# Attention slots of two units: score products on 64-row halves of the array, transposes head by head between filler

## The chip, the cores and the metric

The kernel runs on one core of a Trainium2 chip. The metric is the device time of one execution in microseconds. TensorE (PE) multiplies, with weight loads as instructions of their own (PEld); VectorE (DVE), ScalarE (ACT) and GpSimd (POOL) are the other engines with work; SP, ACT and POOL issue the DMAs. Each engine works through its instructions in their written order and waits on semaphores for the others.

## The reference

One layer on 2048 tokens (a grid of 32 rows by 64 columns) of width 1024: RMSNorm with adaptive shift and scale, one input projection, then two branches whose outputs are joined, projected, gated, added to the input and normalised again. The change is in the neighbourhood attention: 8 heads of 64, and for every token a window of 8 rows by 16 columns of keys.

```
s = jnp.einsum('bhrcd,bhrjkd->bhrcjk', qg, kg) + bias     # scores and relative position bias
s = jnp.where(col_mask[:, None, :], s, -jnp.inf)
p = jax.nn.softmax(s over all keys of the window)
o = jnp.einsum('bhrcjk,bhrjkd->bhrcd', p, vg)
na_out = o * jax.nn.silu(na_z)                             # the gate
out = concatenate([na_out, ml_out]) @ w_out
```

## The kernel before

The program has three stages: the input projections of values and gates with the tables of biases; the mLSTM passes, with the remaining projections (`nq_gen`: z, keys, queries) as filler between their steps; and `phase2`, the attention with the output projection as filler. The fp32 products are made from a high and a low part of each operand: high x high, high x low and low x high.

In `phase2` the tokens are cut into 16 patches of 128 queries (8 rows by 16 columns). A unit is a patch and two heads (`ct`), so there are 64 units, four to a patch; its keys are 264 to 480. The order is written out by hand: `slot(n)` for n = 0 to 65 emits, one after the other, the scores of unit n (`stage_s`), the value products of unit n-2 (`stage_o`), the transposes of unit n-1 (`stage_t`), the loads, the scaling of unit n (`stage_n`) and then `pump(12)`: twelve steps of filler, first the last projections (`pq`), then the output projection of finished patches (`outproj`, tile `y`, 48 matmuls of 512 columns for each patch in two PSUM banks).

- Scores: for each of the two heads, two matmuls over 128 rows into one bank. `kk[ct]` holds, for head j, the high keys on its own 64 rows and the low keys on the other 64; `qhigh` holds the high queries on both halves (a second copy made by DMA, later by `double_q` on DVE), `qlow` the low ones on one half and zeros on the other.
- Softmax: DVE adds the bias table and takes the minimum (line 1346; tables hold the negative), ACT makes the exp with its sum (1347), DVE the reciprocal and the scaling (1356, 1358).
- Transposes: each head's chunks of keys are turned by TensorE into a bank of `pT` (1368; two banks), and ACT copies the bank to SBUF as `pt` (1370).
- Values: `pO` (1383), per chunk two matmuls with 64 columns of the array each, the two heads on the two halves of the output partitions; DVE gates the result into `zs` (1385).
- Output projection: `mix_high` on ACT (1393) and `mix_low` on DVE (1398) split the branch outputs; `y` (1420); DVE adds the residual (1425), ACT squares with a sum into the bank of y (1426), `scale` makes 1/rms with a dozen small DVE operations, `store` scales and writes out. The weights are loaded by `load_w` and split by `split_w` (1321 on ACT, 1322 on DVE) in the first slots (`first`).

PSUM's eight banks: 2 for the fillers (`pp`), 3 `pS`, 2 `pT`, 1 `pO`. The key projections for the lower half of the grid go straight into `kk` in `nq_gen` (885, 886: two ACT and two DVE operations each, on 64 rows), the others by way of DRAM (`kk_jobs`).

Of the kernel before, what the change touches and what calls it, by code (L numbers as in the profile page):

```python
# [62 lines left out]
class Kernel:  # L63
# [780 lines left out]
    def nq_gen(self):  # L844
# [10 lines left out]
        for i, s, g in order:  # L855
# [23 lines left out]
            if kind == "k" and g in lower:  # L879

                for j in range(2):
                    rows, other = slice(j * HD, (j + 1) * HD), slice((1 - j) * HD, (2 - j) * HD)
                    cols = slice(j * T + g * GT, j * T + (g + 1) * GT)
                    hv = self.kk[ct][rows, cols]
# [91 lines left out]
    def kk_jobs(self):  # L976

        flat = lambda t: t.rearrange("p a b -> p (a b)")
        self.kk = [flat(t) for g in (3, 2) for t in (self.hhi[g], self.hlo[g])]

        def load(ct, j, hl):
            src = self.d_kna[hl, ct * P + j * HD : ct * P + (j + 1) * HD, T // 2 :]
            row = j * HD if hl == 0 else (1 - j) * HD
            self.nc.sync.dma_start(self.kk[ct][row : row + HD, j * T + T // 2 : (j + 1) * T].bitcast(F32), src)

        return [[((3, 2)[ct // 2], lambda a=(ct, j, hl): load(*a)) for j in range(2) for hl in range(2)] for ct in range(4)]
# [67 lines left out]
    def ml_pass2(self, ml, h):  # L1054
# [11 lines left out]
        def load_z(gi):  # L1066
            while ("mz", h, gi) not in self.zdone:
                self.pump(1)
            if h == MH - 1 and gi == NG - 1:
                t = self.p2.tile([P, 4, P], F32, tag="pt", bufs=2, name="zt_last")  # L1070
            else:
                t = self.mle.tile([P, 4, CH], F32, tag="zt", bufs=1, name=f"zt_{h}_{gi}")
# [130 lines left out]
    def phase2(self):  # L1203
# [29 lines left out]
        qhigh = [p.tile([P, 2, 2, P], F32R, name=f"qhigh{i}") for i in range(3)]  # L1233
        qlow = [p.tile([P, 2, 2, P], F32R, name=f"qlow{i}") for i in range(3)]
# [14 lines left out]
        def load_q(i):  # L1249
# [3 lines left out]
            hi, lo = qhigh[i % 3], qlow[i % 3]  # L1253
            src = self.d_qna[0, c0 // 2, b].rearrange("(j p) c q -> p j c q", j=2)
            for rows in (slice(0, HD), slice(HD, P))[: 2 if i < 3 else 1]:
                (nc.gpsimd if i < 3 else nc.sync).dma_start(hi[rows].bitcast(F32), src)
            for j in range(2):
                js = slice(j * HD, (j + 1) * HD)
                (nc.gpsimd if i < 3 else nc.sync).dma_start(lo[js, j].bitcast(F32), self.d_qna[1, c0 // 2, b, js])

        def double_q(i):
            hi = qhigh[i % 3]
            nc.vector.tensor_copy(hi[HD:], hi[:HD].bitcast(F32))
# [63 lines left out]
        def stage_s(u):  # L1327
            b, ct = units[u]
            pr, pc, nr, nkc, nk, rpc, nch = geo[b]
            at, c = (u // 2) % 3, ct % 2  # L1330
            pts = []
            sums = few.tile([P, 2], F32, tag="sums", bufs=3, name=f"sums_{u}")
            scores = []
            rs = slice(PR_R0[pr], PR_R0[pr] + nr)
            cs = slice(PC_C0[pc], PC_C0[pc] + nkc)
            for j in range(2):
                ps = pS.tile([P, 512], F32, tag="pS", name=f"pS_{u}_{j}")[:, :nk]
                kv = kk[ct][:, j * T : (j + 1) * T].rearrange("p (r c) -> p r c", c=GRID_W)[:, rs, cs]
                o = ps.rearrange("p (r c) -> p r c", c=nkc)
                nc.tensor.matmul(o, qhigh[at][:, j, c, :], kv, start=True, stop=False)  # L1340
                nc.tensor.matmul(o, qlow[at][:, j, c, :], kv, start=False, stop=True)  # L1341
                scores.append(ps)
            for j, ps in enumerate(scores):
                pt = pbuf[(2 * u + j) % 4]
                mn = few.tile([P, 1], F32, tag="mn", bufs=4, name=f"mn_{u}_{j}")
                nc.vector.tensor_tensor_reduce(pt[:, :nk], ps, tabs[place[u]][j][:, :nk], 1.0, 3e38, ALU.add, ALU.min, mn)  # L1346
                nc.scalar.activation(pt[:, :nk], pt[:, :nk], AF.Exp, bias=mn, scale=-1.0, accum_out=sums[:, j : j + 1])  # L1347
                pts.append(pt)
                if u in follows:
                    load_tab(follows[u], j)  # L1350
            U[u] = (pts, sums)

        def stage_n(u):
# [3 lines left out]
            for j in range(2):  # L1357
                nc.vector.tensor_scalar(pts[j][:, :nk], pts[j][:, :nk], sums[:, j : j + 1], None, ALU.mult)

        def stage_t(u):  # L1360
            pr, pc, nr, nkc, nk, rpc, nch = geo[units[u][0]]
            cs = rpc * nkc
            pts, sums = U.pop(u)
            pT_sb = []
            for j in range(2):
                ps = pT.tile([P, 4, P], F32, tag="pT", name=f"pT_{u}_{j}")
                for i in range(nch):
                    nc.tensor.transpose(ps[:cs, i, :], pts[j][:, i * cs : (i + 1) * cs], self.ident)  # L1368
# [261 lines left out]
```

## Time and profile before

| | |
|---|---|
| median of 3 runs | 1390.58 us (1390.57 to 1395.54) |
| the profiled execution | 1391.12 us, span 1388.9 us |
| mean granted TensorE clock | 0.983 |
| busy: PE, PEld, DVE, ACT, POOL | 1309.5, 1126.1, 830.7, 528.2, 292.6 us |
| first scores | 1011.0 us |
| start of the last value products | 1358.4 us |

Times inside the profile are microseconds from the start of the span; the mean length of one instruction in a group is in ns. Matmul records are pipelined: their lengths overlap, so the distance of their starts is what one costs. A filler's group name (`y`, `pq`) is the tile that it writes.

### The profile page before, as it was taken

What the parts mean: (1) busy time and instruction counts of PE and PEld (TensorE: products, weight loads), DVE (VectorE), ACT (ScalarE), POOL (GpSimd) and SP (SyncE); (2) the same over time, 40 slices, a digit from 0 to 9 for tenths busy, and PEclk for the clock granted to TensorE, in tenths of its full rate; (3) what the DMA queues carried; (4) which work ended last, traced back from release to release, by engine and by line L of the source; (5) the groups of instructions that cost most, each with busy time, mean ns of one, the idle gap of its engine ahead of it and who ended that gap; (6) DMA issues with size and microseconds to landing.
All of it is one profiled execution on the core that took longest, in us unless ns stands there. A gap on an engine that the chain in (4) does not pass through costs nothing.

```text
span 1388.9 us, 23365 instructions
## 1 busy us (share of the span) xinstructions
PE 1309.5 (94%) x8052; PEld 1126.1 (81%) x8052; DVE 830.7 (60%) x2563; ACT 528.2 (38%) x1129; POOL 292.6 (21%) x321
## 2 busy tenths in 40 slices
PE   2989998998999999999999998999998999999996
PEld 2989998898887777888878887788876888888885
DVE  6683323111355569156867877877736777777674
ACT  4642334523222323213323313333345555555551
POOL 4453212424101010001212002212402111112111
PEclk9999999999999999999999999999999999999998
DMA  9798449788457675554776878846697897876862
GB/s 319 227 299 212 122 99 237 186 201 203 120 112 205 149 194 159 170 161 141 194 209 205 246 224 228 231 134 182 181 260 221 187 220 168 204 182 171 193 160 74
DMA packets 269707, 263.67 MB, mean 190 GB/s; under 512 B 33466, under 2 KB 230074, under 8 KB 269590
## 3 DMA queue, kind: packets, MB, share of 16 engines
q1 hardware_dynamic: 178062, 186.45, 50.5%
q0 software_dynamic: 21504, 37.73, 11.0%
q10 hardware_dynamic: 70024, 38.02, 9.7%
q8 instruction: 64, 1.05, 0.3%
q14 instruction: 53, 0.43, 0.1%
HBM read 177.57 MB, written 92.72 MB: 195 GB/s over the span
## 4 chain that ended last, share of the span: by engine, by line
PE 49%; DMA 8%; DVE 4%; issue 3%; ACT 1%; POOL 1%; POOLq 0%; ACTq 0%; SPq 0%; DVEq 0%
PE pq L865 19%; PE y L1420 10%; PE pO L1383 4%; PE pT L1368 3%; DMA tab<-d_t 2%; DMA kv<-d_ck 2%; PE pi L1093 2%; PE pc L429 2%; PE px L1091 2%; PE pc L430 2%; PE pc L431 2%; PE dc L1039 1%; PE pS L1341 1%; PE pS L1340 1%; DMA d_qna<-qst 1%
## 5 line engine op out<-in xcount | busy, mean ns | idle before, releaser
L865 PE MATMUL pq<-hhi,whi_a 128*128 128x512 f32 x512 | 208.7, 408 | 1.3 <-ACT u L773 0.8
L865 PE MATMUL pq<-hlo,whi_a 128*128 128x512 f32 x512 | 209.1, 408 | 0.0
L865 PE MATMUL pq<-hhi,wlo_a 128*128 128x512 f32 x512 | 208.4, 407 | 0.5 <-DVE wlo_a L842 0.5
L1347 ACT ACTIVATE pbuf<-pbuf,mn 128x480 f32<-128x480 f32 (+5 forms) x128 | 76.4, 598 | 105.5 <-DVE mn L1346 105.3
L865 PEld LDWEIGHTS pq<-hhi,whi_a 128*128 128x128 f32 x512 | 97.5, 190 | 19.2 <-ACT u L773 1.2
L865 PEld LDWEIGHTS pq<-hhi,wlo_a 128*128 128x128 f32 x512 | 97.5, 191 | 17.7 <-DVE wlo_a L842 1.0
L865 PEld LDWEIGHTS pq<-hlo,whi_a 128*128 128x128 f32 x512 | 97.5, 190 | 16.4
L1420 PE MATMUL y<-hhi,whi_a 128*128 128x512 f32 x256 | 85.8, 404 | 3.1 <-ACT hhi L1321 2.8
L1420 PE MATMUL y<-hhi,wlo_a 128*128 128x512 f32 x256 | 84.3, 399 | 0.0
L1346 DVE CUSTOM_DVE_ANT_0 pbuf<-pS,tab 128x480 f32<-128x480 f32 (+5 forms) x128 | 65.1, 541 | 29.3 <-PE pS L1341 19.4
L839 POOL TENSOR_TENSOR wlo_a<-rawq,whi_a 128x1024 fp32r<-128x1024 f32 x20 | 48.1, 2407 | 162.9 <-ACT whi_a L838 123.2
L1115 POOL TENSOR_TENSOR hm<-hm,ck 128x128 f32<-128x128 f32 x64 | 26.4, 412 | 263.3 <-DVE hm L1114 178.5
L429 PE MATMUL pvo<-whi_b,hhi 128*128 128x256 f32 x256 | 74.7, 292 | 7.2 <-DVE stvo L499 7.2
L1023 DVE TENSOR_SCALAR wv<-kv,gtile 128x129 f32<-128x129 f32 x120 | 37.9, 323 | 63.0 <-PE dc L1039 33.3
L1096 ACT ACTIVATE num<-px,gtile 128x129 f32<-128x129 f32 x120 | 38.3, 365 | 95.1 <-PE px L1091 75.3
L431 PE MATMUL pvo<-whi_b,hlo 128*128 128x256 f32 x256 | 73.6, 288 | 0.0
L430 PE MATMUL pvo<-wlo_b,hhi 128*128 128x256 f32 x256 | 73.6, 287 | 0.0
L499 DVE TENSOR_TENSOR stvo<-pvo,brow 128x256 f32<-128x256 f32 x64 | 26.5, 420 | 73.6 <-PE pvo L431 59.8
L714 ACT ACTIVATE dec<-dec,gtile 128x128 f32<-128x128 f32 x128 | 42.0, 392 | 69.7 <-POOL dec L710 52.2
L464 DVE TENSOR_TENSOR stv<-pv,brow 128x256 f32<-128x256 f32 x32 | 12.8, 423 | 85.4 <-DMA d_vna<-stv 38.8
L1383 PE MATMUL pO<-pt,v 128*64 128x128 f32 (+3 forms) x832 | 61.3, 283 | 0.5 <-ACT pt L1370 0.5
L1368 PE MATMUL pT<-ident,pbuf 128*128 128x128 f32 (+2 forms) x416 | 59.6, 282 | 0.0
(298 smaller groups left out, 3580.2 us busy)
## 6 DMA issues: line engine op xcount, KB each, us to landing
ck<-d_ck SPq DMA_DIRECT2D x64, 384.5 KB
kv<-d_ck SPq DMA_DIRECT2D x120, 128.5 KB
rawq<-in_w_main_dram SPq DMA_DIRECT2D x28, 512.0 KB
raw<-in_w_main_dram SPq DMA_DIRECT2D x20, 512.0 KB
d_ck<-stvo SPq DMA_DIRECT2D x16, 514.0 KB
x<-in_x_dram SPq DMA_DIRECT2D x16, 512.0 KB
wada<-in_w_ada_dram SPq DMA_DIRECT2D x32, 256.0 KB
dec<-d_mneg SPq DMA_DIRECT2D x32, 256.0 KB
```

What stands on the lines that cost most here:

```text
L429: nc.tensor.matmul(ps, lhi(k), rhi(k), start=(k == 0), stop=False)
L430: nc.tensor.matmul(ps, lhi(k), rlo(k), start=False, stop=False)
L431: nc.tensor.matmul(ps, llo(k), rhi(k), start=False, stop=(k == KT - 1))
L714: nc.scalar.activation(t[:, d, o, :], t[:, d, o, :], AF.Exp, bias=self.cols["g"][:, d, h, c : c + 1])
L839: nc.gpsimd.tensor_tensor(lo[:, :, cs], raw, hi[:, :, cs].bitcast(F32), ALU.subtract)
L865: nc.tensor.matmul(patch_ps(ps) if patch else ps, w, self.htok(h, g, k, patch), start=(k == 0 and n == 0), stop=(k == KT - 1 and n == 2))
L1096: nc.scalar.activation(num[:, d, :], px[:, d, :], AF.Copy, scale=self.cols["inter"][:, d, h, c : c + 1])
L1346: nc.vector.tensor_tensor_reduce(pt[:, :nk], ps, tabs[place[u]][j][:, :nk], 1.0, 3e38, ALU.add, ALU.min, mn)
L1347: nc.scalar.activation(pt[:, :nk], pt[:, :nk], AF.Exp, bias=mn, scale=-1.0, accum_out=sums[:, j : j + 1])
L1368: nc.tensor.transpose(ps[:cs, i, :], pts[j][:, i * cs : (i + 1) * cs], self.ident)
L1383: nc.tensor.matmul(po[j * HD : (j + 1) * HD, :], v[:n, h * HD : (h + 1) * HD], pt[j][:n, i, :], start=(i == 0), stop=(i == nch - 1))
L1420: nc.tensor.matmul(y, m[:, k, :], w[k][:, cs], start=(k == 4 and n == 0), stop=(k == 3 and n == 2))
```

## The change

Slots are of two units, `slot(m)` for m = 0 to 32. It emits the scores of units 2m and 2m+1, the value products of the two units before, both units' softmax, the loads, and then filler and the transposes of one head in turn: 6 filler steps, head, 5, head, 5, head, 4, head, 4 (10, 9, 9, 8, 8 in the first two). The scores are three products over 64 rows for each head, the two heads in turn on rows 0 to 63 and 64 to 127; `kk` and `qs` now hold the parts in plain order, high beside low on the free axis. The queries come by one DMA for each two units, without a second copy (`double_q` and the zeroed `qlow` go). Value products of both units write one bank and are gated by one operation. PSUM: 2 filler, 4 `pS`, 1 `pT`, 1 `pO`. The weight splits of the output projection move from slots 4 to 7 of one unit to slots 2 and 3 of two, four at a time, and the mixes are split where the second head of a pair slot has been turned. The lower keys are written by one ACT and one DVE operation on 128 rows.

```diff
@@ nq_gen
-                for j in range(2):
-                    rows, other = ...
-                    nc.scalar.activation(hv, ps[rows], AF.Identity, bias=bias[rows])
-                    nc.vector.scalar_tensor_tensor(self.kk[ct][other, cols], ps[rows], bias[rows], hv.bitcast(F32), ALU.add, ALU.subtract)
+                hv, lv = (self.kk[ct][:, e * T + g * GT : e * T + (g + 1) * GT] for e in range(2))
+                nc.scalar.activation(hv, ps, AF.Identity, bias=bias)
+                nc.vector.scalar_tensor_tensor(lv, ps, bias, hv.bitcast(F32), ALU.add, ALU.subtract)
@@ phase2
+        def scores(pair):
+            made = {}
+            for u in pair:
...
+                made[u] = [pS.tile([P, 512], F32, tag="pS", name=f"pS_{u}_{j}")[:, :nk] for j in range(2)]
+                for n, (e, f) in enumerate(((0, 0), (1, 0), (0, 1))):
+                    for j, ps in enumerate(made[u]):
+                        js = slice(j * HD, (j + 1) * HD)
+                        o = ps.rearrange("p (r c) -> p r c", c=nkc)
+                        nc.tensor.matmul(o, q[js, e, c, :], keys[f][js], start=(n == 0), stop=(n == 2))
+            for u in pair:
...  (minimum, exp, table load: as in stage_s)
+        def turned(u, j):
+            pr, pc, nr, nkc, nk, rpc, nch = geo[units[u][0]]
             cs = rpc * nkc
+            ps = pT.tile([P, 4, P], F32, tag="pT", name=f"pT_{u}_{j}")
+            for i in range(nch):
+                nc.tensor.transpose(ps[:cs, i, :], U[u][j][:, i * cs : (i + 1) * cs], self.ident)
+            t = p.tile([P, 4, P], F32, tag="pt", bufs=4, name=f"pt_{u}_{j}")
+            nc.scalar.activation(t[:cs, :nch, :], ps[:cs, :nch, :], AF.Copy)
-        pS = self.pool(pss, "pS", bufs=3, space=PSUM)
-        pT = self.pool(pss, "pT", bufs=2, space=PSUM)
+        pS = self.pool(pss, "pS", bufs=4, space=PSUM)
+        pT = self.pool(pss, "pT", bufs=1, space=PSUM)
         first = {
             0: [lambda: nc.sync.dma_start(zs[1], self.d_mix[b0])],
-            3: [lambda: load_w(4), lambda: load_w(5), lambda: load_w(6), lambda: load_w(7)],
-            4: [lambda: split_w(4), lambda: split_w(5), lambda: load_x(b0)],
-            5: [lambda: split_w(6), lambda: split_w(7), lambda: load_z(b1)],
-            6: [lambda: load_m(b1), lambda: split_w(0), lambda: split_w(1), lambda: load_x(b1)],
-            7: [lambda: split_w(2), lambda: split_w(3)],
-            8: [load_fnw],
+            2: [lambda: split_w(4), lambda: split_w(5), lambda: split_w(6), lambda: split_w(7)],
+            3: [lambda: split_w(0), lambda: split_w(1), lambda: split_w(2), lambda: split_w(3), lambda: load_m(b1), lambda: load_x(b1)],
+            4: [load_fnw],
         }
+        last = {1: [lambda: load_w(4), lambda: load_w(5), lambda: load_w(6), lambda: load_w(7)], 2: [lambda: load_x(b0)]}
+        def slot(m):
+            new = (2 * m, 2 * m + 1) if 2 * m < NU else ()
+            old = (2 * m - 2, 2 * m - 1) if m else ()
...
+                scores(new)
+                po = values(old)
+                normalised(new[0])
+                gated(old, po)
+                normalised(new[1])
...
+            fills = [10, 9, 9, 8, 8] if m < 2 else [6, 5, 5, 4, 4]
+            self.pump(fills[0])
+            for n, (u, j) in enumerate([(u, j) for u in new for j in range(2)]):
+                turned(u, j)
+                if n == 1 and m == 2:
+                    self.pump(max(0, self.left) + 1)
+                    self.owed = 0
+                if n == 1:
+                    mixed(ready[:1] if m == 2 else ready)
+                    if m == 2:
+                        load_z(b1)
+                if n % 2:
+                    step()
+                self.pump(fills[n + 1])
```

More of the change, by code (lines that the diff above doesn't have):

```diff
@@ L1231, in phase2 @@
         fnw = []
[L1233 to L1234 removed]
+        qs = [p.tile([P, 2, 2, P], F32R, name=f"qs{i}") for i in range(3)]
         zs = [p.tile([P, 4, P], F32, name="zs"), self.gtile[:, 0:4]]
@@ L1252, in load_q @@
             b, c0 = units[2 * i][0], min(units[2 * i][1], units[2 * i + 1][1])
[L1253 to L1263, printed above, removed]
+            (nc.gpsimd if i < 3 else nc.sync).dma_start(qs[i % 3].bitcast(F32), self.d_qna[:, c0 // 2, b].rearrange("e p c q -> p e c q"))
         def load_v(b, most=4):
@@ L1325, in phase2 @@
         U = {}
[L1327 to L1351, printed above, removed]
```

144 lines of the change are left out of this document (71 added, 73 removed).

## The prediction

> **What bounds the kernel now.** I read the page's engine shares first, then the stretch of the attention slots by windows, TensorE's waits in that stretch, and its timeline.
>
> ```profile
> PE 1309.5 (94%) x8052; PEld 1126.1 (81%) x8052; DVE 830.7 (60%) x2563; ACT 528.2 (38%) x1129; POOL 292.6 (21%) x321
> PE 49%; DMA 8%; DVE 4%; issue 3%; ACT 1%; POOL 1%; POOLq 0%; ACTq 0%; SPq 0%; DVEq 0%
> ```
>
> ```profile
> 1074.90:1358.40 283.50, 283.05 (x1961) 231.14 (x1961) 210.78 (x718) 151.81 (x416) 51.55 (x83) 1.00 0.78 185
> ```
>
> ```profile
> PE pO L1383 <- ACT pt L1370: 0.5, 1, 0.5
> ```
>
> The second is the windows row of the slots from about the tenth unit on (columns: length, then busy time of PE, weight loads, DVE, ACT, POOL, then granted clock): TensorE is busy 283.05 of 283.50 us at clock 1.00. The third is all that it waited there, 0.5 us. So in this stage a microsecond of TensorE work saved is a microsecond gained, and one of waiting added is one lost; DVE (210.8) and ACT (151.8) have room on average, but not at each moment. The other waits of the stage lie in its first slots:
>
> ```profile
> PE y L1420 <- ACT hhi L1321: 2.8, 1, 2.8
> PE y L1420 <- DVE hlo L1322: 0.8, 1, 0.8
> PE pq L865 <- ACT whi_a L841: 0.5, 1, 0.5
> PE pq L865 <- DVE wlo_a L842: 0.5, 1, 0.5
> PE y L1420 <- ACT whi_a L1393: 0.4, 1, 0.4
> ```
>
> That is 5.0 us, from the splits of the output weights and of the last projection weights. Now one slot of 384 keys on TensorE (start, length, line):
>
> ```profile
> 1181.13 0.34 PE L1340 MATMUL pS<-hhi,qhigh 128*128 128x384 f32 x1
> 1181.31 0.34 PE L1341 MATMUL pS<-hhi,qlow 128*128 128x384 f32 x1
> 1181.48 0.34 PE L1340 MATMUL pS<-hhi,qhigh 128*128 128x384 f32 x1
> 1181.66 0.34 PE L1341 MATMUL pS<-hhi,qlow 128*128 128x384 f32 x1
> 1181.93 0.88 PE L1383 MATMUL pO<-pt,v 128*64 128x128 f32 x12
> 1182.73 0.88 PE L1368 MATMUL pT<-ident,pbuf 128*128 128x128 f32 x6
> 1183.36 0.48 PE L1420 MATMUL y<-hlo,wlo_a 128*128 128x512 f32 x1
> ...
> 1184.83 0.39 PE L1420 MATMUL y<-hlo,whi_a 128*128 128x512 f32 x1
> 1185.06 0.62 PE L1420 MATMUL y<-hhi,whi_a 128*128 128x512 f32 x2
> ...
> 1186.20 0.34 PE L1340 MATMUL pS<-hlo,qhigh 128*128 128x384 f32 x1
> ```
>
> The ends overlap, so starts are read: a score matmul takes 0.177, a filler y 0.229, a transpose 0.63/6, about 0.108. The twelve pO records (64 columns, two heads, two records each) take 0.80 us, of which some 0.65 is 0.054 each: half of a transpose's pace, so the two 64-column halves run side by side. Four scores (0.71), pO (0.65), six transposes (0.65) and twelve y (2.75) make 4.77; the slot takes 5.07. The 0.30 left over sits at pS to pO (0.27 instead of 0.18) and at pO to pT: about 0.15 for each change of array shape, two in a slot, 64 slots.
>
> **The change, on TensorE.** All 256 score matmuls together:
>
> ```profile
> 1010.90:1358.40 347.50, 54.64 (x256) 0.99 0.79 195
> ```
>
> (windows, of the score tile alone; second figure busy.) Each group of four overhangs by 0.34 - 0.18 = 0.16, 64 times, so their starts take 54.6 - 10.4 = 44 us; half a microsecond of it was at a low clock, leaving 43.6. The change makes three products of 64 rows per head, 384 matmuls, ordered as pairs on rows 0-63 and 64-127 into two banks. The trace has no 64-row matmul. Bounds: if a pair overlaps as pO's halves do, a unit costs three of these times instead of four, -10.9 us; if not at all, six, +21.8. I take the first, since pO is the nearest row; both ends stay. The Trainium skill's "TensorE: Matmul & The Clock Gate", Part 3, has row tiles overlapping too, 3.07 times for four 32-row tiles; no run here shows it.
>
> Shape changes: before, four in two slots; after, three in a pair slot (y to 64-row scores, scores to values, values to y), since transposes now stand between y of their own shape. 32 x 0.15 = -4.8 to, with the shorter restart, -5.9 us; I take -5.4. If entering the 64-row shape were free, 4.8 more would go. The skill's "TensorEngine Tiling (Array Packing)", Key Properties, says that a change of mode drains the engine: by that rule the entry is paid, as I charge it, and the 0.27 agrees.
>
> Values, transposes and y keep their count. Without cost: double_q (0.42 each) and half the q loads, off the path; the 8 key evacuations lose one ACT and one DVE step each, hidden behind 24 matmuls of 0.23 as before. If that cover were gone they would gain some 0.7 each at most; I book -0.3. Sum on TensorE: -16.6 us.
>
> **The change, in waits.** The price is that pT has one bank instead of two, and that each head's transposes wait for ACT's copy of the previous head's. Before, both heads were turned at once, and nothing on TensorE waited for these copies until the next slot. Now there are 5, 5 and 4 y between, 0.92 to 1.15 us. ACT and DVE are queues: what stands ahead of the copy counts. The rows (mean ns last):
>
> ```profile
> L1347 ACT ACTIVATE pbuf<-pbuf,mn 128x384 f32<-128x384 f32 x16 | 9.7, 610 | 13.8 <-DVE mn L1346 13.7
> L1346 DVE CUSTOM_DVE_ANT_0 pbuf<-pS,tab 128x384 f32<-128x384 f32 x16 | 8.3, 555 | 4.1 <-PE pS L1341 3.5 <-PE pS L1340 0.3 <-DMA tab<-d_t 0.3
> L1358 DVE TENSOR_SCALAR pbuf<-pbuf,sums 128x384 f32<-128x384 f32 x16 | 6.0, 418 | 0.3
> L1370 ACT ACTIVATE pt<-pT 128x384 f32<-128x384 f32 x32 | 13.5, 472 | 0.0
> L1426 ACT ACTIVATE y<-xr 128x512 f32<-128x512 f32 x32 | 19.3, 602 | 56.1 <-DVE xr L1425 56.1
> L1425 DVE TENSOR_TENSOR xr<-xr,y 128x512 f32<-128x512 f32 x32 | 21.9, 686 | 17.0 <-PE y L1420 12.9 <-DMA xr<-in_x_dram 3.8
> L1393 ACT ACTIVATE whi_a<-zs 128x512 fp32r<-128x512 f32 x8 | 4.9, 615 | 0.0
> L1398 DVE TENSOR_TENSOR wlo_a<-wlo_a 128x512 fp32r<-128x512 f32 x8 | 5.5, 686 | 0.0
> L1385 DVE TENSOR_TENSOR zs<-pO,zs 128x128 f32<-128x128 f32 x32 | 9.3, 289 | 3.2 <-PE pO L1383 2.5
> L1321 ACT ACTIVATE hhi<-hlo 128x1024 fp32r<-128x1024 f32 x8 | 8.0, 1050 | 0.0
> ```
>
> Back to back, an operation follows 0.08 to 0.1 sooner than these lengths. I walked the changed order of the queues with them, pair slots 0 to 32.
>
> *A Square ahead of the first copy* (slots 6, 15, 17, 19, 27, 29, 31). Slot 15, 384 keys: first scores done at 0.85; four minima at 0.48 until 2.8; four exps from 1.5 until 4.0; on DVE then two scalings until 3.7, the gating to 4.1 (one of 256 columns, 0.4, for two of 0.29), reciprocal and two scalings until 4.9. Only there stands the residual add: 4.9 to 5.6; Square 5.6 to 6.25; then the copy, 6.7. TensorE: scores 1.2, values to 2.7, 6 y to 4.2, transposes 4.5, 5 y, ready at 5.65. It waits 1.1. With the other sizes: 0.8 to 1.2, together 7.4 us.
>
> *A Square behind both mix copies, ahead of the third head's copy* (slots 4, 14, 16). From the second head's last transpose: its copy to 0.8, mix highs to 1.9 (0.54 apart), mix lows on DVE to about 2.6, the add to 3.3, Square to 3.9, copy to 4.4; TensorE is ready for the fourth head at 2.55. 1.9, 1.9 and 2.35: 6.2 us.
>
> *A Square between copies whose y ended late* (10, 12, 23, 25, 27, 29): 0.1 to 0.8, 2.6 us. *The rsqrt chain, about 2.35 us on DVE, ahead of the next slot's minima* (7, 9): 2.3 us. Sum of the steady slots: +18.5 us. In all others the copy is in time.
>
> *First slots.* The splits of the output weights, four in a row, now stand ahead of the copies in slots 2 and 3: exps end at 3.75, splits (0.95 apart) at 7.5, the copy at 8.1, TensorE is ready at 5.6: 2.5 each. In slot 0 the second head's copy stands behind the last projections' evacuation, which a DMA held, and their weight split:
>
> ```profile
> 1018.50 0.69 ACT L902 ACTIVATE qst<-pq,bcol 128x512 fp32r<-128x512 f32 x1 [5.39 <-DMA d_qna<-qst]
> ...
> 1020.42 1.06 ACT L841 ACTIVATE whi_a<-rawq 128x1024 fp32r<-128x1024 f32 x1 [1.23 <-DVE qst L903]
> ...
> 1045.83 0.69 ACT L902 ACTIVATE qst<-pq,bcol 128x512 fp32r<-128x512 f32 x1 [1.83 <-PE pq L865]
> ...
> 1047.75 0.63 ACT L1393 ACTIVATE whi_a<-gtile 128x512 fp32r<-128x512 f32 x1 [1.23 <-DVE qst L903]
> ```
>
> That split ended at 1021.5, 10.5 us after the first scores (1011.0); the copy follows at 10.9, TensorE is ready at 8.4: 2.5. In slot 2 the first y comes right behind the last projection, with no scores and values between: from evacuation to the end of the mix copy it is 2.55, with the last matmul's end 2.8. Sum 10.3, less the 5.0 of before: +5.3. If the weights' DMAs (SP, now issued nearer to the splits) land late, more.
>
> *Clock.* After a wait of 2 us TensorE ran at half pace:
>
> ```profile
> 899.48 0.49 PE L1039 MATMUL dc<-wv,kv 128*128 128x129 f32 x2 [2.14 <-DVE wv L1023]
> ...
> 900.51 0.63 PE L865 MATMUL pq<-hhi,wlo_a 128*128 128x512 f32 x1
> 900.93 0.63 PE L865 MATMUL pq<-hhi,whi_a 128*128 128x512 f32 x1
> ```
>
> 0.42 instead of 0.23 apart. It lasted until 903.4 in the timeline, 3.4 us at half speed, so 1.7 us each time. Five of the waits above are over 2 us and two at 1.9; I count six, take half as lost in the next wait anyway, and take off 2 for the one of before: +3, between 0 and +8.
>
> **The sum.** -16.6 + 18.5 + 5.3 + 3 = +10.2 us. The profiled execution took 1391.1 (span 1388.9), 0.5 over the median of the three runs, 1390.6; from the median it is 1400.8, in round numbers 1401 us. The tail (last y, residual, store) is unchanged.
>
> **Rivals.** *The waits do not form (faster).* Place: ACT's copy of the first or third head in the steady slots. If the minima, exps and scalings run closer than I walked, or scores and values take longer on TensorE, the copy ends before the 5 y do. At no steady wait it is -16.6 + 5.3 + 1.5 = -9.8: 1381 us. It decides from the point where all waits and clock together, 27 as I have them, stay under 16.6; at half the steady waits and half the clock it is about zero. For it: the cover of 1.15 us is near the 1.1 that is missing, and DVE and ACT are a quarter and half idle on average. Against: the add stands behind all scalings in the queue, whatever their pace, and a shorter score block brings TensorE to the copy sooner.
>
> *Pairs do not overlap.* Then scores cost +21.8 in place of -10.9; the waits shrink by some 5, as TensorE comes later: 1401 + 32.7 - 5, about 1428 us. For it: no 64-row matmul in the trace. Against: pO's halves.
>
> *Weight loads of a pair follow one another.* Each pair needs two loads of 128 columns; transposes, one such load each, stand 0.108 apart, so a pair would take at least 0.215, which only 480 keys hide (0.177 x 480/384 is 0.22; 288 keys make 0.13). Three times 0.04 to 0.09 for each of the 48 smaller units, about +9, of which 2 fall into waits: 1408 us. pO's loads run in pairs, against it. The skill's "TensorE: Matmul & The Clock Gate", LDWEIGHTS, gives columns / 1.2 ns whatever the rows, 107 ns here by an estimate, and so this case if they queue; the transposes' pace agrees with that figure.
>
> *Gain and waits cancel.* Three quarters of the waits: 1394 us, no change to measure.
>
> **Chances.** Forecast (waits as walked) 0.50; cancel 0.18; waits do not form 0.14; loads in line 0.10; no overlap 0.08. The measurement tells about 0.5%, 7 us, from no change, that is 1383.6 to 1397.5. Faster: most of the third case, 0.11. Same: the cancelling case but for 0.02, the rest of the third, 0.07 of the forecast's own lower edge: 0.26. Slower 0.63. Range 1383 to 1416: it takes in the first, second and fourth cases and the late DMA, and leaves out no overlap and half of the third; the forecast's own range is 1394 to 1411.
>
> **What would show it.** Right: score matmuls starting in twos a few ns apart, three twos per unit at the old spacing; TensorE's waits on ACT's copy (pT behind pt) near 25 us in all, the longest in slots 0 to 4, then 14 and 16; half-clock stretches there. Wrong: twos 0.18 apart or 0.21 per two (the second and third rivals), or TensorE busy throughout the steady slots (the first); a wait on DMA at the splits would add to mine.

## The result, and the profile after

The changed kernel takes 1417.85 us (median of 6 runs, 1412.28 to 1421.94) against 1394.43 us for the kernel before (6 runs, 1390.57 to 1401.71): a ratio of 1.0156, 95% interval 1.0128 to 1.0185, some 22 us slower. The forecast was +10 us, 1401 us from a kernel before of 1390.6; the range ended at 1416. The sign came as forecast and the size did not. Of the 17 us between 1401 and the measured time some 4 come from the kernel before, which is slower in these six runs than in the first three; the other 13 are the change's. The page of the changed kernel, engine shares and the chain that ended last:

```profile
PE 1304.6 (92%) x8180; PEld 1110.5 (78%) x8180; DVE 803.7 (57%) x2494; ACT 529.4 (37%) x1121; POOL 286.1 (20%) x309
PE 40%; DVE 10%; DMA 8%; issue 4%; ACT 3%; SPq 1%; POOL 1%; ACTq 0%; POOLq 0%; DVEq 0%
```

TensorE is still what bounds the kernel, but DVE and ACT have a larger part in the chain (10% and 3%; before, 4% and 1%). The windows from the first scores to the last y ("the stretch" from here on; length, then busy time of PE, weight loads, DVE, ACT, POOL, clock), before and after:

```profile
1011.00:1376.85 365.85, 360.45 (x2380) 292.55 (x2378) 253.93 (x828) 185.71 (x493) 61.80 (x99) 0.99 0.77 189
```

```profile
1024.86:1404.00 379.14, 355.50 (x2508) 276.28 (x2507) 234.46 (x767) 192.54 (x492) 62.58 (x100) 0.99 0.72 179
```

The stretch is 13.3 us longer: TensorE works 5.0 us less and stands 18.2 us more. What it waited for there, and the clock in two parts of it:

```profile
PE pT L1354 <- ACT pt L1356: 16.4, 16, 2.5
PE pT L1354 <- DVE pbuf L1346: 3.8, 4, 1.3
PE y L1411 <- ACT whi_a L1384: 2.6, 1, 2.6
PE y L1411 <- ACT wlo_a L1384: 0.7, 1, 0.7
```

```profile
1064.80:1110.90 46.10, 41.17 (x279) 31.56 (x279) 27.68 (x85) 23.48 (x60) 10.73 (x17) 0.93 0.71 184
1165.00:1238.00 73.00, 67.03 (x484) 51.41 (x484) 45.24 (x147) 36.40 (x92) 12.12 (x20) 0.98 0.70 169
```

The waits for ACT's copy are there, and three stretches of 3.4 us at a granted clock of one half (two in the first row, one in the second). The rest of the loss lies ahead of the stretch, where nothing had been booked (timeline of TensorE):

```profile
1014.06 0.40 PE L865 MATMUL pq<-hhi,wlo_a 128*128 128x512 f32 x1
1019.90 0.77 PE L865 MATMUL pq<-hhi,whi_a 128*128 128x512 f32 x1 [5.44 <-DVE qst L900]
1020.46 0.63 PE L865 MATMUL pq<-hlo,whi_a 128*128 128x512 f32 x1
```

Before, the last 29 projection matmuls ahead of the first scores took 6.7 us; now they take 14.3: a wait of 5.4 us and then half clock (0.42 us apart). Below, this wait with the half clock behind it is called the stall. Together 13.3 + 7.6 = 20.9 us, close to the 22 of the ratio. The two profiled executions differ by 27.1; the other 6.3 had gathered earlier, where only the keys' evacuations and loads were changed. I take that for chance, which is not shown: the 256th-last projection matmul stands at 970.3 before and 976.6 after, and between 958.0 and 977.9 in the other profiles below, which come from several chips.

Why a copy is late, in the seventeenth slot (slot 16; ACT, then TensorE):

```profile
1220.14 0.49 ACT L1356 ACTIVATE pt<-pT 128x384 f32<-128x384 f32 x1 [1.00 <-PE pT L1354]
1220.53 0.62 ACT L1384 ACTIVATE wlo_a<-wlo_a 128x512 fp32r<-128x512 f32 x1
1221.05 0.62 ACT L1384 ACTIVATE wlo_a<-gtile 128x512 fp32r<-128x512 f32 x1
1223.11 0.60 ACT L1417 ACTIVATE y<-xr 128x512 f32<-128x512 f32 x1 [1.44 <-DVE xr L1416]
...
1223.74 0.47 ACT L1356 ACTIVATE pt<-pT 128x384 f32<-128x384 f32 x1
```

```profile
1222.05 0.40 PE L1411 MATMUL y<-hlo,whi_a 128*128 128x512 f32 x1
1224.26 0.55 PE L1354 MATMUL pT<-ident,pbuf 128*128 128x128 f32 x3 [1.81 <-ACT pt L1356]
1224.56 0.71 PE L1411 MATMUL y<-hhi,whi_a 128*128 128x512 f32 x2
```

ACT stands idle for 1.44 us at the Square (L1417), which waits for DVE's residual add. The copy behind it (L1356, at 1223.74) could have run at once, since its transposes ended at 1221.5. TensorE waits for that copy.

### The profile page after: what moved, and what is told of

It is laid out like the page before. It is cut to its first block, busy times and chain, and to the rows that moved or that the text cites. A ratio compares the mean times of both kernels' runs of the same rounds, so it can differ in the third digit from the quotient of the medians.

```text
span 1416.4 us, 23348 instructions
## 1 busy us (share of the span) xinstructions
PE 1304.6 (92%) x8180; PEld 1110.5 (78%) x8180; DVE 803.7 (57%) x2494; ACT 529.4 (37%) x1121; POOL 286.1 (20%) x309
## 3 DMA queue, kind: packets, MB, share of 16 engines
q8 instruction: 65, 1.06, 0.3%
## 4 chain that ended last, share of the span: by engine, by line
PE 40%; DVE 10%; DMA 8%; issue 4%; ACT 3%; SPq 1%; POOL 1%; ACTq 0%; POOLq 0%; DVEq 0%
PE pq L865 18%; PE y L1411 9%; PE pT L1354 3%; PE pS L1326 2%; DMA kv<-d_ck 2%; PE pO L1369 2%; DVE acc_q L808 2%; PE pi L1089 2%; DMA tab<-d_t 2%; PE px L1087 2%; PE dc L1035 1%; DMA d_mix<-zt 1%; DMA rawq<-in_w_main_dram 1%; PE a L1074 1%; SPq L551 1%
## 5 line engine op out<-in xcount | busy, mean ns | idle before, releaser
L1356 ACT ACTIVATE pt<-pT 96x384 f32<-96x384 f32 (+3 forms) x128 | 65.6, 512 | 80.1 <-PE pT L1354 80.1
L1411 PE MATMUL y<-hhi,whi_a 128*128 128x512 f32 x256 | 92.8, 421 | 2.6 <-ACT whi_a L1384 2.6
L1411 PE MATMUL y<-hhi,wlo_a 128*128 128x512 f32 x256 | 90.3, 412 | 0.7 <-ACT wlo_a L1384 0.7
L1354 PE MATMUL pT<-ident,pbuf 128*128 128x128 f32 (+2 forms) x416 | 68.8, 279 | 20.3 <-ACT pt L1356 16.4
L1354 PEld LDWEIGHTS pT<-ident,pbuf 128*128 128x128 f32 (+2 forms) x416 | 49.5, 137 | 47.6 <-ACT pt L1356 30.0
```

The source lines that it names most:

```text
L1354: nc.tensor.transpose(ps[:cs, i, :], U[u][j][:, i * cs : (i + 1) * cs], self.ident)
L1356: nc.scalar.activation(t[:cs, :nch, :], ps[:cs, :nch, :], AF.Copy)
L1411: nc.tensor.matmul(y, m[:, k, :], w[k][:, cs], start=(k == 4 and n == 0), stop=(k == 3 and n == 2))
```

## The experiments

Ratios are to the kernel before on the same chip, with 95% intervals. The stretch is read from each run's profile, from the first scores to the start of the last y: 378.9 us for the changed kernel, 365.6 before. Edits are shown in part; "..." marks what is left out.

**Ring of five banks** (`e1_ring`):

```diff
-        pS = self.pool(pss, "pS", bufs=4, space=PSUM)
-        pT = self.pool(pss, "pT", bufs=1, space=PSUM)
+        pS = self.pool(pss, "pS", bufs=5, space=PSUM)
...
-            ps = pT.tile([P, 4, P], F32, tag="pT", ...)
+            ps = pS.tile([P, 512], F32, tag="pS", ...).rearrange("p (i q) -> p i q", q=P)
```

> The changed kernel, but scores and transposes rotate through five banks of one ring in place of four for scores and one for transposes, so no head's transposes wait for the copy of the head before. Theory (the one bank of the transposes is what costs): the 16.4 us in 16 waits on ACT's copy go, each with about 0.2 us of refilling the pipeline of matmuls, and the half-clock stretches that follow the two longest (1.7 us each) with them; the waits for DVE's scaling (3.8) and for the weight splits (3.3) stay: 18 to 22 us less than the changed kernel, about 1397 us. Rival (ACT and DVE as queues are the limit): the waits come back one step later, on DVE's scaling or on a bank of the ring, and less than 6 us is won, above 1411 us.

1.0061 (1.0035 to 1.0087), 13 us less than the changed kernel; the stretch is 363.2, 15.7 less and 2.4 under the kernel before. The waits of its stretch:

```profile
PE pT L1354 <- DVE pbuf L1346: 9.5, 8, 1.9
PE y L1411 <- ACT whi_a L1384: 3.2, 1, 3.2
PE y L1411 <- ACT wlo_a L1384: 0.7, 1, 0.7
PE y L1411 <- ACT y L1417: 0.3, 1, 0.3
```

The waits for ACT's copy are gone; 5.7 us more are spent on waits for DVE's scaling, mostly with the 1/rms chain or a late table ahead of it. The theory holds for the one bank, but the gain is 13 us and not its 18 to 22: in part the waits came back one step later, as the rival said.

**No Square** (`e7_nosquare`):

```diff
-                    nc.scalar.activation(y, x[:, cs], AF.Square, accum_out=ssq[:, i : i + 1])
+                    nc.gpsimd.memset(ssq[:, i : i + 1], 1.0)
```

> The changed kernel without ACT's Square (the sum of squares is left out and set to 1; the residual add on DVE stays). Theory of the walk (a Square, held by the residual add behind all scalings, stands ahead of the copy that the next transposes need): the waits on ACT's copy fall from 16.4 to some 5 us (those of the weight splits in the third and fourth slot stay), with their restarts 11 to 13 us less: about 366 us from the first scores to the last y, 1406 us in all. Rival (the copies are late because DVE's scaling is late, or ACT is too full in general): the waits fall by 3 us or less, 375 us or more for the stretch, 1414 us or more.

1.0060 (1.0037 to 1.0082), the stretch 364.5:

```profile
PE pT L1354 <- DVE pbuf L1346: 5.4, 7, 1.5
PE pT L1354 <- ACT pt L1356: 4.7, 2, 2.5
```

This kernel leaves out the sum of squares, so its output is not normalised by it. Of 16 waits for the copy two are left, both behind the weight splits. It is the Square's place in ACT's queue, as walked: the add on DVE is still there, but with no Square between them it does not hold the copies.

**The two halves of the change apart.** `e4_rows64` is the kernel before with the 64-row products and their layout, in slots of one unit:

```diff
...
-                nc.tensor.matmul(o, qhigh[at][:, j, c, :], kv, start=True, stop=False)
-                nc.tensor.matmul(o, qlow[at][:, j, c, :], kv, start=False, stop=True)
+            for n, (e, f) in enumerate(((0, 0), (1, 0), (0, 1))):
+                for j, ps in enumerate(scores):
+                    nc.tensor.matmul(o, qs[at][js, e, c, :], keys[f][js], start=(n == 0), stop=(n == 2))
```

> The kernel before, with one part of the change alone: three score products over 64 rows for each head, by turns, in slots of one unit as before, with the queries and keys laid out for it. From the first scores to the last y it took 365.6 us before. Theory (pairs save a quarter of the scores' time, some 10 us, and entering the 64-row shape from y, which was no change of shape before, costs about 0.15 in each of 64 slots, 9.6 us): 364 to 367 us for this stretch, no gain. Rival (entering is free): 355 to 357 us. Rival (entering and leaving cost 0.25 together with the longer first pair): 371 us or more. The start may stall as in the changed kernel, since the queries' copies are gone here too: the whole 1391 to 1400 us by the theory.

`e8_rows128` is the reverse: slots of two units with the four 128-row products, the zeroing and the copies, but with two query buffers in place of three.

```diff
-                for n, (e, f) in enumerate(((0, 0), (1, 0), (0, 1))):
-                    for j, ps in enumerate(made[u]):
-                        nc.tensor.matmul(o, q[js, e, c, :], keys[f][js], start=(n == 0), stop=(n == 2))
+                for j, ps in enumerate(made[u]):
...
+                    nc.tensor.matmul(o, qhigh[(u // 2) % 2][:, j, c, :], kv, start=True, stop=False)
+                    nc.tensor.matmul(o, qlow[(u // 2) % 2][:, j, c, :], kv, start=False, stop=True)
```

> The slots of two units alone: the changed kernel with the four 128-row score matmuls of before, their layout of keys and queries, the zeroing and the second copies (two query buffers in place of three, for room). Theory (64-row pairs win 10.9 us of matmul time, but entering their shape from y costs about 0.2 a slot, 6 in 32 slots; the stall ahead of the first scores comes from the missing copies and zeroing on POOL): about 381 us from the first scores to the last y against 378.9, and no wait of 5 us ahead of the first scores: 1391 + 15, about 1406 us. Rival (the products are worth their whole 10.9): 390 us for the stretch. Rival for the stall (it comes from the new order of slots): the wait of 5 to 6 us stays.

They give 1.0065 (1.0044 to 1.0086) and 1.0156 (1.0127 to 1.0185). The windows of the stretch, e4 and e8:

```profile
1016.22:1381.10 364.88, 360.45 (x2508) 275.84 (x2507) 239.14 (x799) 185.24 (x492) 61.84 (x99) 1.00 0.72 186
```

```profile
1005.50:1389.30 383.80, 360.08 (x2380) 289.01 (x2378) 247.68 (x796) 193.62 (x493) 67.68 (x107) 0.99 0.73 180
```

| stretch; wait ahead of the first scores | four 128-row products | three 64-row products |
|---|---|---|
| slots of one unit | 365.6; none | 364.7; 6.0 |
| slots of two units | 383.6; none | 378.9; 5.4 |

In slots of one unit the products bring nothing: TensorE is busy for 360.45 us with them and without them. In slots of two they save 4.6 of busy time. The slots alone cost 14 to 18 us. (e8 has 2.4 us of waiting for a late table in one slot, the changed kernel 1.05 there, so its stretch is some 1.3 too long.)

e4 shows that the products' layout brings the stall without the new slots: its stretch is 0.9 shorter than before, and yet it loses 9 us by its ratio. That e8 has no stall says less, since its two buffers change the loads too. On POOL the third query load has to wait for the first scores, and the second patch's values stand behind it:

```profile
1006.89 1.21 POOL L1256 DMA_DIRECT2D qhigh<-d_qna  x2 [10.70 <-PE pS L1340]
```

So e8 does not rule out that the new slots, too, have a part in the stall.

**Order of the products** (`e3_byhead`): three products of head 0 ahead of three of head 1.

```diff
-                for n, (e, f) in enumerate(((0, 0), (1, 0), (0, 1))):
-                    for j, ps in enumerate(made[u]):
+                for j, ps in enumerate(made[u]):
+                    for n, (e, f) in enumerate(((0, 0), (1, 0), (0, 1))):
```

> The changed kernel, with the three score products of one head emitted ahead of the three of the other, in place of by turns. Theory (two neighbouring products overlap if they lie on different rows, and products are taken in order): in a slot only the last of a head and the first of the next overlap, so nine times in place of six for twelve products: 31.7 us of starts become 47, +16 us, less some 3 that come out of waits for copies: about 1431 us. Rival (no overlap in this order): twelve times, +32, about 1446 us. Rival (each half of the rows has a queue of its own, order is free): 1418 us.

1.0200 (1.0150 to 1.0250), the stretch 379.0 against 378.9: the third case. Timeline of TensorE in a slot of 384 keys:

```profile
1184.76 0.81 PE L1326 MATMUL pS<-hhi,qs 64*128 64x384 f32 x6
1185.41 0.71 PE L1326 MATMUL pS<-hlo,qs 64*128 64x384 f32 x6
1186.04 1.65 PE L1369 MATMUL pO<-pt,v 128*64 128x128 f32 x26
```

Twelve products in 1.28 us, as by turns (1.27 below). In the trace they start in twos 10 ns apart (3 to 4 by turns). The rows do not name the head, but the two products of a unit that raise TensorE's semaphore, the last of each head, stand together in the third two. So TensorE takes the second head's product ahead of the first head's second one. That the build kept the written order is seen in the same marks: by turns the second head's last product raises the semaphore by one, right behind the first head's, and in e3 it adds a larger step in all 64 units.

**The stall ahead of the first scores.** ACT's split of the weights waits for their load (512 KB, on SP), and the evacuation that TensorE needs stands behind it. Before and after:

```profile
ACT whi_a L841 <- DMA rawq<-in_w_main_dram: 4.5, 1, 4.5
```

```profile
ACT whi_a L841 <- DMA rawq<-in_w_main_dram: 11.7, 1, 11.7
```

SP's waits for such loads (total, times, longest), before and after:

```profile
SPq L830 <- DMA rawq<-in_w_main_dram: 9.8, 2, 5.8
```

```profile
SPq L830 <- DMA rawq<-in_w_main_dram: 17.0, 2, 13.1
```

Of the twelve query loads on POOL three larger ones are left, and the zeroing is gone, so POOL's next loads come sooner. The first load of the first patch's values and the first of the second patch's, before and after:

```profile
999.42 2.00 POOL L1276 DMA_DIRECT2D v<-d_vna  x3
1007.22 0.70 POOL L1276 DMA_DIRECT2D v<-d_vna  x1 [0.28 <-DMA v<-d_vna]
```

```profile
1001.49 1.36 POOL L1261 DMA_DIRECT2D v<-d_vna  x2
1005.53 1.99 POOL L1261 DMA_DIRECT2D v<-d_vna  x3
```

SP issued the weights' load at 996.78 and 1003.10. So the first values started 2.6 us behind it before and 1.6 ahead of it now, and the second patch's 10.4 behind it, when the weights had landed, and now 2.4. The DMA queues show what this does. Before, SP's queue moved 0.47 MB, nearly all of the load, from 999 to 1002 us, while POOL's moved 0.07. Now from 1009 to 1016 us SP's moves 0.19 MB, the last third of the load, and POOL's 1.31. Four edits move these loads:

`e2_sp`: the first patch's values and gates and the third queries go to SP's queue, behind the weights.

```diff
-        load_v(b0)
-        load_z(b0)
+        load_v(b0, queue=nc.sync)
+        load_z(b0, nc.sync)
         load_q(2)      # nc.sync from the third on, not the fourth
```

> The changed kernel, but the first patch's value and gate loads and the third query load are issued by SP, behind the load of the second-last projection weights, in place of POOL. Theory (with the copies of the queries and the zeroing gone, POOL issues these loads some 4 us sooner, they take the DMA engines while the weights' 512 KB are on the way, these land after 13 us in place of 6, and TensorE stands 5.4 us and then runs 4 us at half clock): the weights land in some 6 us, TensorE does not wait ahead of the first scores, 7 us less than the changed kernel, about 1411 us. Rival (the late landing was chance, or is set by something else): no change, 1418 us. Second rival: the values now come late for the first value products and the stall only moves by 10 us: no change either, but with a wait on DMA in the second slot.

1.0146 (1.0089 to 1.0202): the wait fell to 1.3, but 4.8 us came up earlier, at a transpose that waits for ACT (`ht`), since DVE had waited 5.1 us for a store ahead of it. There is no gain: the stall had only moved, to an earlier place and not to the later one of the second rival.

`e5_gate`: a small POOL operation on the split weights ahead of those loads.

```diff
+        turn = self.wslot[0][0][:, KT - 1, P - 1 : P + 1].bitcast(F32)
+        nc.gpsimd.tensor_tensor(few.tile([P, 2], F32, name="gate"), turn, turn, ALU.subtract)
         load_v(b0)
         load_z(b0)
         load_q(2)
```

> The changed kernel, but on POOL the first patch's value and gate loads and the third query load stand behind a 2-column operation that reads the weights of a late projection after their split, so they start only when that weight load has landed. Theory (the stall ahead of the first scores, 5.4 us of waiting and some 2 us of half clock, comes from these loads sharing the DMA engines with the 512 KB of weights): the wait goes, the weights land in about 6 us, and the time falls by 7 to 8 us, to about 1410 us; from the first scores to the last y it stays at 379. Rival (other transfers hold the weights, the queue of POOL is innocent): the wait stays at 5 to 6 us and the time at 1418. Second rival (values late): the wait moves into the first two slots, no gain.

1.0186 (1.0135 to 1.0238), the wait 5.5. The edit did not do what it says: the loads stood ahead of the operation on POOL in the built order, which here is not the written one, so the run tells nothing of the loads.

`e9_late`: the operation stands in the first slot, ahead of the second patch's values, and reads the first scaled probabilities; `e12_first`: the first patch's loads stand behind it too, and it reads the split weights (in one diff, e12's lines as comments):

```diff
+            if m == 0:
+                seen = U[0][0][:, :2]      # e12: the weights after their split
+                nc.gpsimd.tensor_tensor(few.tile([P, 2], F32, name="gate"), seen, seen, ALU.subtract)
+                # e12: load_v(b0), load_z(b0), load_q(2) moved here
             for n in new:
                 loads(n)
```

> The changed kernel, but the value loads of the second patch (three of 240 KB, and those behind them on POOL) stand behind a 2-column POOL operation that reads the first scaled probabilities of the first slot, so they cannot start before the first scores. Theory (these loads hold the last 60 KB of the weights' load for 7 us; in the kernel before POOL's many small query loads kept them back): the weights land about 6 us after their issue, TensorE's wait of 5.4 to 7 us ahead of the first scores goes with its half-clock time, 7 to 8 us less in all: a ratio of about 1.010 to the kernel before in place of 1.0156; the stretch from the first scores to the last y stays at 376 to 379. Rival (other transfers hold the weights, and the query loads matter in another way): the wait stays, 1.0156.

> The changed kernel, but all of POOL's loads behind the query and table loads of the first two slots (the first patch's values and gates, the third queries, and all that follows) stand behind a 2-column POOL operation that reads the late projection weights after their split. Theory (both groups of loads together hold the weights' load; the second group alone gave back 1.3 to 2.8 us of the wait): the weights land in some 6 us, TensorE's wait ahead of the first scores falls under 1 us and no half-clock stretch follows: a ratio near 1.008 to the kernel before. Rival (what holds the weights is the query, table and ACT traffic that stays): the wait stays near 4 us and the ratio near 1.0104. Second rival (values now late): a wait for DMA at the first values.

e9: 1.0104 (1.0050 to 1.0157), the ratio that was expected, but by luck: the wait did not go, it fell to 4.2, and the 29 matmuls take 13.9. With the same edit they take 11.4 and 12.8 in e10 and e11 below; with those loads left alone 14.3 to 16.6 (the changed kernel, e1, e3, e5, e6, e7). So some of the stall, between the means 2.7 us, is from the second patch's values. e12: 1.0172 (1.0124 to 1.0220), slower, though the weights now land as before and the 29 matmuls take 6.8 us again. ACT's and TensorE's waits there:

```profile
ACT whi_a L841 <- DMA rawq<-in_w_main_dram: 4.7, 1, 4.7
```

```profile
PE pT L1354 <- ACT pt L1356: 6.8, 1, 6.8
```

So both groups of loads together make the stall. But held back they take nothing off the time: in the first slot ACT waits 8.7 us for the store of the projected queries, the second head's copy stands behind that, and TensorE waits 6.8 us for the copy, in the place where the prediction had put 2.5. In the kernel before ACT waited for such a store too (5.39 us), and it cost TensorE 1.0. That the held loads are what delays the store is argued from their place in time, not shown.

**Towards a version that beats both.** `e6_full`: ring, the gate of e5 (which again stands behind the loads), the 1/rms chain and the store in mid-slot, splits spread over two slots, last projections ended later.

```diff
...
+                if n == 1 and m != 2:
+                    mixed(ready)
...
-                if n % 2:
+                if n == 1:
                     step()
+                    step()
+                for fn in spread.pop((m, n), ()):      # one split_w to a head in slots 2 and 3
+                    fn()
                 self.pump(fills[n + 1])
...
+            if m == 2:
+                self.pump(max(0, self.left) + 1)
+                self.owed = 0
+                mixed(ready)
```

> The changed kernel with three repairs together: the ring of five banks; the held loads; and DVE's and ACT's late work moved: the chain of 1/rms and the store stand in the middle of a slot, not ahead of the next slot's minima, the eight weight splits are spread one to a head over two slots, and the last projections end with the third slot, so that scores and values cover the first mix. Theory (all that was lost is waits, and the score pairs and shape changes together win a little): from the first scores to the last y about 353 us (363.2 with the ring alone, less 3.2 at the first y, some 7 of waits for DVE's scaling and their restarts), no stall ahead of them, in all 10 to 14 us less than the kernel before, about 1378 us. Rival (the moved chain and splits now delay the residual adds and scalings): 360 us or more for the stretch, 1386 us or more in all.

1.0173 (1.0114 to 1.0232), the stretch 375.2: 21.5 us of waits for DVE's scaling, and the wait ahead of the first scores is still 6.0. In the slot looked at (1307 to 1312 us on DVE) chain and store together run straight into the next slot's minima; this is the rival.

`e10_ringlate`: ring and held loads of e9. `e11_steps`: with it, chain and store moved apart:

```diff
             if new:
                 normalised(new[1])
+                step()
...
-                if n % 2:
+                if n == 1:
                     step()
```

> The ring of five banks for scores and transposes and the held value loads together. Theory (both losses are independent): 363 us from the first scores to the last y and no stall ahead of them: 1.0061 - 0.0055, a ratio of 1.000 to 1.001 to the kernel before, about as fast. Rival (held value loads come late once the slots are shorter): waits for DMA in the first slots, 1.004 or more.

> As the one before, and the chain of 1/rms and the store are emitted behind the scalings of a slot and behind the second head's transposes, not ahead of the next slot's minima. Theory (with the ring, TensorE's remaining waits for scalings in slots 5, 7, 9 and 30, 4.5 us, come from that chain ahead of the minima; those in slots 21 and 26 come from the tables' DMA and stay): 358 to 360 us for the stretch, a ratio of 0.996 to 0.998. Rival (the chain now delays the residual adds and with them the banks of y): waits on y for ACT's Square, no gain, 1.000 or more.

e10: 1.0033 (1.0005 to 1.0062), between its theory (1.000 to 1.001) and its rival (1.004). e11: 0.9965 (0.9940 to 0.9991), faster than both, and than the kernel before by a third of a percent, with an interval that ends just under 1. The stretch is 352.8, less than the 358 to 360 expected, and TensorE waits there 5.0 us in all:

```profile
PE y L1411 <- ACT whi_a L1384: 3.2, 1, 3.2
PE pT L1354 <- DVE pbuf L1346: 1.1, 2, 0.9
PE y L1411 <- ACT wlo_a L1384: 0.7, 1, 0.7
```

`e13_all`: e11 with the loads held as in e12 (the same lines). `e14_flush`: the last projections end with the third slot.

```diff
                 turned(u, j)
-                if n == 1 and m == 2:
-                    self.pump(max(0, self.left) + 1)
...
                 self.pump(fills[n + 1])
+            if m == 2:
+                self.pump(max(0, self.left) + 1)
+                self.owed = 0
             if m == 2 or not new:
-                mixed(ready[1:] if m == 2 else ready)
+                mixed(ready)
```

> Ring of five banks, moved 1/rms chain and store, and the loads held as in the run above. Theory: the faster version of before (0.9965) less the remaining wait of 4.2 us and its half clock: 0.992 to 0.994 of the kernel before. Rival (the wait stays, or the values come late): 0.996 or more.

> As the run above, and the last projections end with the third slot, so that the fourth slot's scores and the values stand between the last projection matmul and the first y, and cover the evacuation and the first mix. Theory (the wait of 3.2 us at the first y and the half clock behind it go): some 4 us less than the run above, 0.989 to 0.991. Rival (the copy of the fourth head or the mix is late in ACT's queue, behind the four weight splits): no gain, 0.992 or more.

0.9972 (0.9946 to 0.9998) and 1.0025 (1.0001 to 1.0048). In e13 the stall is gone, and 3.4 us of waiting for the last weights' split stand in the first slot; its stretch is 358.6, 5.9 longer than in e11: no gain. In e14 the first y no longer waits, but heads' transposes wait for scalings (7.0 us in 7 waits) and a score for its bank (2.6). I take it that later y changed which slots meet which add, which is not shown. Both times fall in their rivals' ranges.

## Why the prediction was wrong in size

*The step that failed: half the queries' loads "without cost, off the path".* The term was put at nothing and measured +7.6 us. Fewer and larger loads on POOL are off TensorE's path themselves, but they let other loads start earlier, and these slow the load of a late projection's weights, whose split stands ahead of the evacuation that TensorE needs. e4 shows that it comes with the layout, and e12 that it goes when POOL's loads are held. The prediction named late DMAs only at the output weights' splits. The Trainium skill's "DMA: Bandwidth & Descriptors", "Issuing engines are not separate DMA queues", says that transfers of all issuing engines share 16 DMA engines and interleave; the 13.1 us against 5.8 agree.

*The term that was mis-sized: changes of shape, -5.4 forecast, 0 to -2 found.* The count of three in a slot was right, the price was not. A slot of 384 keys begins in the changed kernel, and the end of another's values:

```profile
1190.00 0.40 PE L1411 MATMUL y<-hhi,wlo_a 128*128 128x512 f32 x1
1190.33 0.80 PE L1326 MATMUL pS<-hhi,qs 64*128 64x384 f32 x6
1190.97 0.70 PE L1326 MATMUL pS<-hlo,qs 64*128 64x384 f32 x6
1191.60 0.33 PE L1369 MATMUL pO<-pt,v 128*64 128x128 f32 x2
```

```profile
1181.05 1.97 PE L1369 MATMUL pO<-pt,v 128*64 128x128 f32 x32
1182.95 0.50 PE L1411 MATMUL y<-hlo,wlo_a 128*128 128x512 f32 x1
1183.30 0.62 PE L1411 MATMUL y<-hhi,wlo_a 128*128 128x512 f32 x2
```

From y to scores 0.33 in place of 0.23; six pairs in 1.27 in place of 6 x 0.177 = 1.06; sixteen pairs of values in 1.90 in place of 1.74; the first y 0.35 in place of 0.23. That is 0.10 + 0.21 + 0.16 + 0.12 = 0.59 a slot, nearly 0.2 for each change: 19 us in 32 slots, as much as 64 times 0.30 before. Entering the 64-row shape is paid at both ends, at the last y and in the first pair; e4, with 64 entries, shows the pairs' gain eaten whole. A second reading is e11, where TensorE waits 5.0 us in the stretch (5.4 before) at the same clock:

```profile
1017.80:1370.80 353.00, 347.95 (x2508) 277.78 (x2507) 233.44 (x767) 191.38 (x492) 64.15 (x103) 0.99 0.75 194
```

It is busy 12.5 us less than before. The pairs make 10.9 of that, which leaves 1.6 for the changes of shape. So TensorE's own work fell by 12.5 and not by 16.6.

*Scores: right.* The two products of a pair start 3 to 4 ns apart and a pair 0.18 behind the one before, three pairs per unit: -10.9 us less the entries above. "No overlap" and "weight loads in line" are out.

*Waits for the copies: right, somewhat too large.* 23.6 us of idle time in the stretch against 28.8 walked (18.5 and 10.3). The largest stood where they were walked: the Square behind the mixes in slots 4, 14 and 16, 1.29, 1.81 and 1.81 (1.9, 1.9 and 2.35 walked); the rsqrt chain in 7 and 9, 2.5 in all (2.3); the Square ahead of the first copy in its seven slots, 5.3 in all (7.4); the splits in 2 and 3, 2.2 and 2.5 (2.5 each); the first y 2.6 (2.8). In slot 0 there was none; I take it that the stall had given the store time. e1 and e7 show bank and Square as the two conditions. Rivals "waits do not form" and "gain and waits cancel" are out.

*Not booked: the restart.* A wait costs more than its idle time: the last y before it is not overlapped, 0.39 in place of 0.23 (1222.05 to 1224.26 is 2.21 for 1.81 of waiting), nearly 0.2 here, and there are 22 waits. *Clock:* three half-clock stretches for six counted, 1.7 us more than before.

The sum as found for the stretch: idle time +18.2, TensorE's own work -12.5 (by e11), clock +1.7, and as the remainder some +6 of restarts, about 0.3 for each of the 18 waits that it has more than e11: +13, against a forecast of +10.2. With the stall it is 21. So the stall (+7.6), restarts (+6) and shape changes (+4) were missing or too small, and waits (-5.6) and clock (-1.3) were too large. That the stretch came within 3 us of the forecast is luck: these errors nearly cancel.

## What to carry to other kernels

When a step frees an engine that others pace, or a queue of loads, ask what moves up into the room: here values moved ahead of weights and TensorE paid. A buffer taken away is paid for where a slow engine's queue stands between write and read: list what is ahead of the read in that queue, slot by slot; such a walk found the waits to a fifth, and a ring of banks shared by two uses took most of them away. Count a change of array shape at both of its ends.

## What the hardware showed that was not expected

TensorE did not keep to the program's order, which the description of the engines ahead of the prediction says of every engine. Products on different row halves do not need to be neighbours in the program: three of one head and then three of the other ran in twos 10 ns apart, at the same pace (e3, stretch 379.0 against 378.9). The Trainium skill's "TensorE: Matmul & The Clock Gate", Part 3, says that matmuls start and end strictly in program order, and by that rule e3 would have been slower; the run decides against it here.
